# Prompt attention as half-array matmuls: 64 rows of the array for the scores, 64 columns for the values

## The chip, the cores and the metric

The kernel runs on one core of a Trainium2 chip. The metric is device time in microseconds, the median of several runs of the whole program. Three runs of the kernel before gave 1952.34 (median), 1952.07 and 1954.67 us.

The engines are named as in the profile: PE is the matrix engine, PEld its weight loads, DVE, ACT and POOL the vector, scalar and general engines, SP the queue that issues most of the transfers. A matmul multiplies a stationary operand (loaded as weights) with a moving operand that streams through it.

## The reference

One layer of a hybrid decoder is computed for a prompt of 256 tokens and for 8 single decode tokens: a half-step FFN, a mixing stage, a second half-step FFN, a final norm. Mixing has a group of attention heads beside a group of RWKV heads. The change touches the attention of the prompt:

```
qb = q.reshape(B, nb, BLOCK, N_KV_HEADS, GQA_GROUP, HEAD_DIM)
kc = concatenate([kp[:, :-1], kp[:, 1:]])      # the block before, and its own
s = einsum('...qhgd,...khd->...hgqk', q, k) * HEAD_DIM**-0.5 + bias
s = where(valid, s, -inf)
m = maximum(max(s), sink);  p = exp(s - m)
denom = sum(p) + exp(sink - m)
out = einsum('...hgqk,...khd->...qhgd', p / denom, v)
```

There are 16 query heads of 64 dimensions and 4 key/value heads, so four query heads share one key head. The 256 tokens form two blocks of 128. The second block's queries see 256 keys, the first block's only their own 128.

## The kernel before

The 264 columns of every activation are the 256 prompt tokens and the 8 decode tokens, and features lie along the 128 partitions. Every large product goes through `gemm`: weights come from memory as fp32, ACT makes a rounded copy `hi`, DVE the rest `lo`, and three matmuls of 264 columns (hi by hi, hi by lo, lo by hi) stand for one full product. These write the PSUM tiles called `acc`. All smaller products, attention among them, use plain fp32 operands and write PSUM tiles called `m`; each of them appears in the trace as two matmul records, one for each of the two passes that an fp32 matmul takes here.

The mixing stage multiplies by `w_in` tile by tile (`win`) in the order of the table `SEQ`: RWKV batches, then two key tiles and two value tiles (kind `kv`), then eight query tiles (kind `q`). Work that follows on a tile is a Python generator (`attend`, `prep`, `chain` and others) which moves forward one step at a time between chunks of the next `gemm` (`tick`). A scheduler then places every instruction on its engine with costs of its own, so the final order of the matmuls on PE is not the order in which the code is written.

A query tile `t` holds two heads, one in partitions 0 to 63 and one in 64 to 127 (`HALF`), and belongs to key pair `p = t // 4`. `attend(t, q)` does for it:

- scores (lines 796 to 798): for each head `h`, one matmul for the second block against 256 keys and one for the first block against 128 keys. The stationary operand is a block of `q` with all 128 partitions. So that only one head counts, the keys lie in two tiles per pair, `kT[p][0]` and `kT[p][1]`, each with the other head's 64 partitions set to zero (lines 926 to 931).
- bias, softmax and three transposes for each head (lines 799 to 816).
- values (lines 819 to 822): for each head, one matmul with the first 128 values for 256 queries and one with the second 128 values for the last 128 queries. The stationary operand is `Vt[p][:, i, :]` with the columns of both heads, so the output has 128 partitions of which 64 are wanted. ACT copies these out, one copy for each head (line 824).

Blocks that outlive a stage are taken by `blk(tag, n)` as `n` rows of 320 elements; block `y` has 16 elements more at its end. In the rows of the profile `kv` is the block that holds the keys and values, `o` the block that holds the `q` tiles, and the `t` in `m<-t,kv` are the probabilities.

Of the kernel before, what the change touches and what calls it, by code (L numbers as in the profile page):

```python
# [10 lines left out]
ALU = mybir.AluOpType  # L11
AX = mybir.AxisListType

P = 128
NP = 256
NB = 8
T = NP + NB
# [7 lines left out]
HALF = (slice(0, 64), slice(64, 128))  # L25
# [5 lines left out]
ROW = 320  # L31
# [21 lines left out]
def body(tc, I, O):  # L53
    nc = tc.nc
    V, A, G, TE, SP = nc.vector, nc.scalar, nc.gpsimd, nc.tensor, nc.sync
# [3 lines left out]
    def uid(s):  # L59
        cnt[0] += 1  # L60
        return f"{s}{cnt[0]}"

    def tt(e, out, a, b, op):
        return e.tensor_tensor(out=out, in0=a, in1=b, op=op)  # L64

    def stt(out, a, s, b, op0, op1):
        return V.scalar_tensor_tensor(out=out, in0=a, scalar=s, in1=b, op0=op0, op1=op1)  # L67
# [11 lines left out]
    def mm(out, lhsT, rhs, start=True, stop=True, **k):  # L79
        return TE.matmul(out, lhsT, rhs, start=start, stop=stop, **k)  # L80
# [16 lines left out]
    def spawn(g):  # L97
        tasks.append(g)
        return g

    def pause(n):
        for _ in range(n):
            yield

    with ExitStack() as ctx:
        cp = ctx.enter_context(tc.tile_pool(name="cp", bufs=1))
        sp = ctx.enter_context(tc.tile_pool(name="sp", bufs=1))
# [3 lines left out]
        cur = [None]  # L111

        def blk(tag, n, dt=F32):
            t = sp.tile([P, n * ROW + (16 if tag == "y" else 0)], dt, tag=tag, bufs=1, name=uid(tag))
            return [t[:, j * ROW:j * ROW + T] for j in range(n)]

        def pairs(*rows):
# [2 lines left out]
        def tmp(shape=(P, T), dt=F32):  # L120
            pool, n = cur[0]
            return pool.tile(list(shape), dt, tag="t", bufs=n, name=uid("t"))
# [4 lines left out]
        def mp():  # L127
            return pp.tile([P, 512], F32, tag="m", bufs=NM, name=uid("m"))
# [42 lines left out]
        def vc(i):  # L171
            return vec[:, i:i + 1]
# [189 lines left out]
        def mixing_body(mx, n2, n3, XD, XR):  # L362
            def fix(shape, name):
                return mx.tile(list(shape), F32, name=name)

            def ring(shape, tag, bufs):
                return mx.tile(list(shape), F32, tag=tag, bufs=bufs, name=uid(tag))

            def load(src, shape):
                t = ring(shape, "ld", NLD)  # L370
                SP.dma_start(t, src)
                return t
# [10 lines left out]
            rs = fix((P, T), "rs")  # L383
# [366 lines left out]
            kT, Vt = [None] * 2, [None] * 2  # L750
# [39 lines left out]
            def attend(t, q):  # L790
                p = t // 4
                G.tensor_copy(qd[:, p, :, t % 4], q[:, NP:T])
                bs = [load(I["bias"][(2 * p + h) * 4 + t % 4], (P, 256)) for h in range(2)]
                yield
                spp = [mp(), mp()]
                for h in range(2):
                    mm(spp[h][:, 0:256], q[:, P:NP], kT[p][h][:, 0:NP])
                    mm(spp[h][:, 256:384], q[:, 0:P], kT[p][h][:, 0:P])
                sc = [(tmp((P, 256)), tmp((P, P))) for h in range(2)]
                mxv = ring((P, 4), "mxv", 6)  # L800
                for h, sps in enumerate(spp):
                    s1, s0 = sc[h]
                    head = (2 * p + h) * 4 + t % 4
                    for s, a, b, j in ((s1, sps[:, 0:256], bs[h], 0), (s0, sps[:, 256:384], bs[h][:, P:256], 1)):
                        V.tensor_tensor_reduce(out=s, in0=a, in1=b, op0=ALU.add, op1=ALU.max, scale=1.0,  # L805
                                               scalar=vc(VSK + head), accum_out=mxv[:, 2 * h + j:2 * h + j + 1])
                softmax([x for y in sc for x in y], mxv, [vc(VSK + (2 * p + h) * 4 + t % 4) for h in range(2)], 4)
                yield
                yield from pause(PW[4])
                for s1, s0 in sc:  # L810
                    tp = mp()
                    TE.transpose(tp[:, 0:P], s0, ident)  # L812
                    TE.transpose(tp[:, P:2 * P], s1[:, 0:P], ident)  # L813
                    TE.transpose(tp[:, 2 * P:3 * P], s1[:, P:256], ident)  # L814
                    A.copy(s1, tp[:, 0:256])
                    V.tensor_copy(s0, tp[:, 256:384])
                yield
                pt = sc
                op = mp()
                for h in range(2):  # L820
                    mm(op[:, h * 256:h * 256 + 256], Vt[p][:, 0, :], pt[h][0], True, False)
                    mm(op[:, h * 256 + P:h * 256 + 256], Vt[p][:, 1, :], pt[h][1], False, True)
                for h in range(2):
                    A.copy(q[HALF[h], :NP], op[HALF[h], h * 256:h * 256 + 256])
                mixed[8 + t] = q

            sd = fix((P, P), "sd")
# [79 lines left out]
            for kind, i in SEQ:  # L907
                if kind == "b":
                    bt = newbatch(i)
                    for k in range(BATCH[i]):  # L910
                        p = bt.p0 + k
                        x = [shifted(2 + 3 * p + j, tmp()) for j in range(3)]
                        spawn(prep(p, bt, k, *x))
                    bat.append(spawn(chain(bt)))
                    bts.append(bt)
                    if len(bat) == len(BATCH):
                        A.dma_start(O["sh"], shc)
                elif kind == "kv":
                    w, p = i // 2, i % 2
                    ps = win(LKV + i)  # L920
                    if w:
                        xs = (tmp(),)
                        with tc.high_priority():
                            tt(V, xs[0], ps[:, :T], rs, ALU.mult)
                    else:
                        xs = (kvb[2 * p], kvb[2 * p + 1])
                        kT[p] = xs
                        for h in range(2):
                            G.memset(xs[h][HALF[1 - h], :], 0.0)
                            with tc.high_priority():  # L930
                                tt(V, xs[h][HALF[h], :], ps[HALF[h], :T], rs[HALF[h], :], ALU.mult)
                    spawn(kvtask(w, p, xs))
                else:
                    ps = win(LKV + 4 + i)
                    q = ob[i]
                    with tc.high_priority():
                        stt(q, ps[:, :T], 0.125, rs, ALU.mult, ALU.mult)
                    att.append(spawn(attend(i, q)))
                    if i % 4 == 3:
                        scores.append(spawn(dec_scores(i // 4)))  # L940
                    if len(att) == 8:
                        att.append(spawn(dec_attend(list(att), scores)))
# [19 lines left out]
            for pi, ks in enumerate(PASS):  # L962
# [15 lines left out]
                for o in range(KD):  # L978
                    ps = acc()
# [58 lines left out]
        kvb, ob, yb = blk("kv", 6), blk("o", 8), blk("y", 8)  # L1038
# [107 lines left out]
```

## Time and profile before

| what | value |
|---|---|
| median of three runs | 1952.34 us |
| the profiled execution | 1952.57 us |
| its span in the profile | 1950.8 us |
| PE busy | 1935.6 us |
| DVE busy | 1307.7 us |
| ACT busy | 1035.9 us |
| POOL busy | 260.2 us |

The span runs from the first to the last instruction; the profiled execution's own time is 1.77 us more. Times in the profile's rows count from the start of the span. The first FFN takes the time up to about 757 us, the mixing stage from there to about 1145 us, the second FFN the rest.

A row of a group reads: line, engine, operation, output and operands (the moving one first), for a matmul the rows by the columns of the array that are in use, the moving operand's shape, and the count; then busy time and the mean of one. The mean is the time from the start of a matmul to the end of its result, which is longer than the distance between two starts, because matmuls follow each other in a pipeline. For the cost of a matmul the distance between starts in the timeline is the measure.

### The profile page before, as it was taken

The numbers are of one execution on the slowest core, as the hardware profiler recorded it, in microseconds if no ns is written. First come the engines' busy times: TensorE is split into PE (matmuls) and PEld (weight loads), VectorE is DVE, ScalarE is ACT, GpSimd is POOL, SyncE is SP. The second block draws the span as 40 slices with busy tenths as digits, with TensorE's granted clock in tenths as the row PEclk, the third lists the DMA queues.
The fourth block names the chain that finished last, engine by engine and source line by source line (L and its number), as shares of the span: only waits on it lengthen the run. The fifth ranks groups of instructions, "written<-read, shape, count | busy, mean of one in ns | idle before, by whom it ended". The sixth has DMA issues, their size and how long they took to land.

```text
span 1950.8 us, 45522 instructions
## 1 busy us (share of the span) xinstructions
PE 1935.6 (99%) x17131; PEld 1919.6 (98%) x17131; DVE 1307.7 (67%) x2591; ACT 1035.9 (53%) x2069; POOL 260.2 (13%) x382
## 2 busy tenths in 40 slices
PE   9999999999999999999999999999999999999998
PEld 9999999999999999999999999999999999999998
DVE  5865555655556567799768877866666666666655
ACT  5644444444454456665577645644444444444445
POOL 0401101010010112231102100210101001010012
PEclk9999999999999999999999999999999999999999
DMA  7666666655656567555545655566666666666654
GB/s 241 178 195 193 185 195 197 184 188 178 189 182 186 183 194 232 165 169 157 149 128 163 188 157 183 175 186 188 190 192 193 186 193 189 192 193 184 194 180 149
DMA packets 220958, 358.10 MB, mean 184 GB/s; under 512 B 34866, under 2 KB 74434, under 8 KB 220738
## 3 DMA queue, kind: packets, MB, share of 16 engines
q1 hardware_dynamic: 214226, 346.59, 59.5%
q10 hardware_dynamic: 6512, 8.61, 1.4%
q8 instruction: 134, 2.20, 0.4%
q14 instruction: 86, 0.70, 0.1%
HBM read 347.48 MB, written 9.70 MB: 183 GB/s over the span
## 4 chain that ended last, share of the span: by engine, by line
PE 98%; DVE 1%; ACT 0%; DMA 0%; issue 0%; DVEq 0%; SPq 0%; ACTq 0%
PE acc L80 89%; PE m L80 8%; DMA x<-in_x 0%; DMA t<-dr 0%; DVE y L64 0%; PE m L535 0%; DVE lo L64 0%; ACT t L74 0%; ACT hi L137 0%; PE m L812 0%; PE m L493 0%; PE m L528 0%; PE m L813 0%; PE m L814 0%; DVE t L805 0%
## 5 line engine op out<-in xcount | busy, mean ns | idle before, releaser
L64 DVE TENSOR_TENSOR lo<-raw,hi 128x512 fp32r<-128x512 f32 (+1 forms) x1288 | 875.7, 683 | 523.4 <-ACT hi L137 496.2
L137 ACT CAST hi<-raw 128x512 fp32r<-128x512 f32 (+1 forms) x1288 | 777.1, 607 | 803.3 <-PE acc L80 735.5
L80 PE MATMUL acc<-x,hi 128*128 128x264 f32 x4840 | 900.0, 287 | 1.6 <-DVE st L64 1.3
L80 PEld LDWEIGHTS acc<-x,hi 128*128 128x128 f32 x4840 | 753.2, 189 | 4.9 <-ACT t L74 1.4
L80 PE MATMUL acc<-x,lo 128*128 128x264 f32 x2420 | 692.6, 286 | 0.2 <-DVE lo L64 0.2
L80 PE MATMUL acc<-h,hi 128*128 128x264 f32 x2752 | 495.1, 284 | 0.0
L80 PEld LDWEIGHTS acc<-x,lo 128*128 128x128 f32 x2420 | 458.5, 190 | 1.7 <-DVE lo L64 0.4
L80 PEld LDWEIGHTS acc<-h,hi 128*128 128x128 f32 x2752 | 424.4, 189 | 0.0
L80 PE MATMUL acc<-h,lo 128*128 128x264 f32 x1376 | 387.2, 284 | 0.0
L80 PEld LDWEIGHTS acc<-h,lo 128*128 128x128 f32 x1376 | 259.2, 189 | 0.0
L64 POOL TENSOR_TENSOR t<-t,t 128x264 f32<-128x264 f32 x74 | 80.3, 1085 | 1096.4 <-DVE t L64 950.3
L80 PE MATMUL acc<-y,hi 128*128 128x264 f32 x648 | 123.9, 285 | 0.0
L80 PE MATMUL acc<-o,hi 128*128 128x264 f32 x648 | 120.0, 283 | 0.0
L80 PE MATMUL acc<-kv,hi 128*128 128x264 f32 x582 | 109.8, 284 | 0.0
L80 PEld LDWEIGHTS acc<-y,hi 128*128 128x128 f32 x648 | 101.4, 189 | 0.1
L80 PEld LDWEIGHTS acc<-o,hi 128*128 128x128 f32 x648 | 100.1, 189 | 0.0
L67 DVE SCALAR_TENSOR_TENSOR x<-acc,x 128x264 f32<-128x264 f32 x192 | 81.0, 426 | 24.5 <-PE acc L80 23.6
L80 PE MATMUL acc<-y,lo 128*128 128x264 f32 x324 | 92.0, 284 | 0.0
L80 PE MATMUL acc<-o,lo 128*128 128x264 f32 x324 | 91.7, 283 | 0.0
L80 PEld LDWEIGHTS acc<-kv,hi 128*128 128x128 f32 x582 | 90.2, 189 | 0.1
L64 DVE TENSOR_TENSOR t<-acc,t 128x264 f32<-128x264 f32 x156 | 67.4, 432 | 33.1 <-PE acc L80 32.9
L80 PE MATMUL acc<-kv,lo 128*128 128x264 f32 x291 | 82.8, 284 | 0.0
(300 smaller groups left out, 1635.5 us busy)
## 6 DMA issues: line engine op xcount, KB each, us to landing
raw<-in_gu SPq DMA_DIRECT2D x688, 256.0 KB, 3.4
raw<-in_dn SPq DMA_DIRECT2D x224, 256.0 KB, 2.9
raw<-in_win SPq DMA_DIRECT2D x152, 256.0 KB, 3.4
raw<-in_dn SPq DMA_DIRECT2D x160, 192.0 KB, 2.7
raw<-in_wout SPq DMA_DIRECT2D x64, 256.0 KB, 3.4
xsp<-x ACTq DMA_DIRECT2D x16, 132.0 KB, 3.7
x<-xsp SPq DMA_DIRECT2D x16, 132.0 KB, 3.6
ld<-in_sT SPq DMA_DIRECT2D x16, 128.0 KB, 4.2
```

The lines of the kernel that those rows point to most:

```text
L64: return e.tensor_tensor(out=out, in0=a, in1=b, op=op)
L67: return V.scalar_tensor_tensor(out=out, in0=a, scalar=s, in1=b, op0=op0, op1=op1)
L80: return TE.matmul(out, lhsT, rhs, start=start, stop=stop, **k)
L137: A.copy(hi[:, :w], raw[:, :w])
```

## The change

Scores: a matmul reads only the 64 partitions of its head, from `q` and from a single key tile, so that it uses 64 rows of the array. Values: a matmul has only the 64 columns of its head as weights and writes only that head's 64 partitions, so that it uses 64 columns of the array. In both places the loop now goes over the column range first and over the two heads inside it. One ACT copy takes the finished 128 partitions out. The key tile of a pair is written whole, by one DVE multiplication, with no zeroed halves. The 16 spare elements lie behind block `e` in place of block `y`.

```
@@ blk @@
-            t = sp.tile([P, n * ROW + (16 if tag == "y" else 0)], dt, tag=tag, bufs=1, name=uid(tag))
+            t = sp.tile([P, n * ROW + (16 if tag == "e" else 0)], dt, tag=tag, bufs=1, name=uid(tag))
@@ attend @@
                 spp = [mp(), mp()]
-                for h in range(2):
-                    mm(spp[h][:, 0:256], q[:, P:NP], kT[p][h][:, 0:NP])
-                    mm(spp[h][:, 256:384], q[:, 0:P], kT[p][h][:, 0:P])
+                for a, b, n in ((0, P, NP), (NP, 0, P)):
+                    for h in range(2):
+                        r = HALF[h]
+                        mm(spp[h][:, a:a + n], q[r, b:b + P], kT[p][r, 0:n])
...
                 op = mp()
-                for h in range(2):
-                    mm(op[:, h * 256:h * 256 + 256], Vt[p][:, 0, :], pt[h][0], True, False)
-                    mm(op[:, h * 256 + P:h * 256 + 256], Vt[p][:, 1, :], pt[h][1], False, True)
-                for h in range(2):
-                    A.copy(q[HALF[h], :NP], op[HALF[h], h * 256:h * 256 + 256])
+                for i, a in ((0, 0), (1, P)):
+                    for h in range(2):
+                        r = HALF[h]
+                        mm(op[r, a:NP], Vt[p][:, i, r], pt[h][i], i == 0, i == 1)
+                A.copy(q[:, :NP], op[:, :NP])
@@ the keys @@
-                        xs = (kvb[2 * p], kvb[2 * p + 1])
-                        kT[p] = xs
-                        for h in range(2):
-                            G.memset(xs[h][HALF[1 - h], :], 0.0)
-                            with tc.high_priority():
-                                tt(V, xs[h][HALF[h], :], ps[HALF[h], :T], rs[HALF[h], :], ALU.mult)
+                        xs = (kvb[p],)
+                        kT[p] = xs[0]
+                        with tc.high_priority():
+                            tt(V, xs[0], ps[:, :T], rs, ALU.mult)
```

The scheduler puts the matmuls of the mixing stage in a new order. Three places on PE show what matters. A row gives the line, the operation, output and operands with running numbers, and the shape of the output; `m_...<-kv,o` is a score matmul (the two heads of a tile write two tiles with numbers of their own), `m_...<-t,kv` a value matmul, `acc` a matmul of a gemm. The score rows look alike before and after since their output has 128 partitions in both, but after the change each uses 64 rows of the array.

The first place is the second query tile's scores, before:

```order
L80 MATMUL m_13972<-C,t_13869 88x2 x3
L80 MATMUL m_14072<-kv_110,o_111 128x256
L80 MATMUL m_14072<-kv_110,o_111 128x128
L80 MATMUL acc_14326<-x_107,lo_14359 128x264
L80 MATMUL acc_14326<-x_107,hi_14358 128x264
L80 MATMUL m_14073<-kv_110,o_111 128x256
L80 MATMUL m_14073<-kv_110,o_111 128x128
L80 MATMUL m_14191<-sgl,ld_13858 128x264
```

And of the change:

```order
L80 MATMUL m_13966<-C,t_13863 88x2 x3
L80 MATMUL m_14066<-kv_110,o_111 128x256
L80 MATMUL m_14066<-kv_110,o_111 128x128
L80 MATMUL acc_14320<-x_106,lo_14323 128x264
L80 MATMUL acc_14320<-x_106,hi_14322 128x264 x2
L80 MATMUL acc_14320<-x_106,lo_14323 128x264
L80 MATMUL m_14067<-kv_110,o_111 128x256
L80 MATMUL m_14067<-kv_110,o_111 128x128
L80 MATMUL m_14185<-sgl,ld_13852 128x264
```

The two heads' matmuls still stand apart, with matmuls of the gemm between them, although the code alternates the heads.

The second place is the scores of the fifth query tile, before:

```order
L80 MATMUL acc_15319<-x_108,hi_15413 128x264
L80 MATMUL m_15381<-kv_110,o_111 128x256
L80 MATMUL m_15381<-kv_110,o_111 128x128
L80 MATMUL m_15382<-kv_110,o_111 128x256
L80 MATMUL m_15382<-kv_110,o_111 128x128
L80 MATMUL acc_15319<-x_108,hi_15413 128x264
```

And of the change:

```order
L493 MATMUL m_15341<-C,t_15113 128x128 x2
L80 MATMUL m_15371<-kv_110,o_111 128x256
L80 MATMUL m_15372<-kv_110,o_111 128x256
L80 MATMUL m_15371<-kv_110,o_111 128x128
L80 MATMUL m_15372<-kv_110,o_111 128x128
L80 MATMUL acc_15309<-x_108,hi_15403 128x264
```

Here the heads do alternate, and the four matmuls stand together.

The third place is the end of the first tile's values beside the fourth tile's scores, before:

```order
L80 MATMUL acc_14480<-x_109,lo_14617 128x264
L80 MATMUL m_14345<-t_13902,kv_110 128x128
L80 MATMUL m_14345<-t_13903,kv_110 128x256
L80 MATMUL m_14376<-kv_110,o_111 128x256
L80 MATMUL m_14376<-kv_110,o_111 128x128
L80 MATMUL m_14345<-t_13904,kv_110 128x128
L80 MATMUL m_14427<-qb_10433,ld_14428 128x2x4 x2
```

And of the change:

```order
L80 MATMUL acc_14473<-x_107,hi_14519 128x264 x2
L80 MATMUL m_14339<-t_13896,kv_110 64x128
L80 MATMUL m_14369<-kv_110,o_111 128x256
L80 MATMUL m_14339<-t_13898,kv_110 64x128
L80 MATMUL m_14369<-kv_110,o_111 128x128
L80 MATMUL m_14420<-qb_10433,ld_14421 128x2x4 x2
```

Matmuls on 64 columns and matmuls on 64 rows now take turns here, one at a time, between matmuls on the whole array.

## Prediction

> **What bounds the kernel now.** I read the page first (busy times), then a table by stage, then the waits, then the timeline of PE around the attention.
>
> ```profile
> PE 1935.6 (99%) x17131; PEld 1919.6 (98%) x17131; DVE 1307.7 (67%) x2591; ACT 1035.9 (53%) x2069; POOL 260.2 (13%) x382
> PE 98%; DVE 1%; ACT 0%; DMA 0%; issue 0%; DVEq 0%; SPq 0%; ACTq 0%
> 0.00:757.00 757.00, 755.45 (x6267) 754.66 (x6268) 464.76 (x788) 383.36 (x693) 98.01 (x107) 1.00 0.64 193
> 757.00:1145.00 388.00, 383.23 (x4244) 368.45 (x4243) 316.26 (x889) 252.57 (x654) 68.77 (x176) 0.99 0.56 161
> 1145.00:1951.00 806.00, 796.90 (x6624) 796.46 (x6623) 526.68 (x915) 399.93 (x723) 93.43 (x99) 1.00 0.62 186
> ```
>
> PE is busy for 99% of the span and makes up 98% of the chain that ended last. The mixing stage, the fourth line, is no exception: 383.23 of 388.00 us (the first number is the stretch, the second PE). So what the change does to the time is what it does to the length of PE's own queue in that stage, plus PE's few waits there:
>
> ```profile
> PE m L80 <- issue: 2.4, 1, 2.4
> PE acc L80 <- DVE st L64: 1.3, 1, 1.3
> PE m L80 <- ACT t L504: 1.1, 1, 1.1
> 943.80:947.20 3.40, 3.40 (x17) 3.40 (x17) 0.69 (x1) 1.44 (x4) 0.00 (x0) 0.50 0.53 152
> 1100.80:1104.20 3.40, 3.40 (x17) 3.40 (x16) 3.02 (x13) 1.69 (x4) 0.73 (x1) 0.50 0.38 117
> ```
>
> Three waits, 4.8 us together, and two stretches of 3.4 us in which the granted clock (the 0.50) is half, which lose about 1.7 us each: 8.2 us is all that better order in this stage could win back beyond PE's work.
>
> **Part 1, the matmuls themselves.** The attention of the prompt is these four groups, 128 records, two for each of 64 matmuls:
>
> ```profile
> L80 PE MATMUL m<-t,kv 128*128 128x256 f32 x32 | 10.0, 395 | 0.0
> L80 PE MATMUL m<-kv,o 128*128 128x256 f32 x32 | 9.8, 388 | 0.0
> L80 PE MATMUL m<-t,kv 128*128 128x128 f32 x32 | 6.7, 292 | 0.0
> L80 PE MATMUL m<-kv,o 128*128 128x128 f32 x32 | 6.1, 274 | 0.0
> ```
>
> Their place in PE's queue is read from starts, for one tile's scores:
>
> ```profile
> 978.20 0.28 PE L80 MATMUL acc<-x,lo 128*128 128x264 f32 x1
> 978.32 0.29 PE L80 MATMUL acc<-x,hi 128*128 128x264 f32 x1
> 978.44 1.47 PE L80 MATMUL m<-kv,o 128*128 128x256 f32 x8
> 979.67 0.37 PE L80 MATMUL acc<-x,hi 128*128 128x264 f32 x1
> 979.88 0.28 PE L80 MATMUL acc<-x,lo 128*128 128x264 f32 x1
> ```
>
> Starts of gemm matmuls lie 0.12 us apart. The second one after the scores starts at 979.88, so the scores take 979.88 - 0.12 - 978.44 = 1.32 us of the queue: four passes of 256 and four of 128 columns, 0.22 and 0.11 us each. One head's pair of matmuls is 0.66 us, a tile's scores and values 2.64 us, all eight tiles 21.1 us.
>
> Do two half-array matmuls run at once? The trace of before has such pairs, on 64 rows (`m<-kr,bk`) and on 64 columns (`m<-uv,BT`, `m<-gm,uv`):
>
> ```profile
> 815.98 0.63 PE L80 MATMUL m<-t,C 128*128 128x280 f32 x2
> 816.54 2.06 PE L80 MATMUL m<-kr,bk 64*128 64x128 f32 x32
> 818.53 0.39 PE L80 MATMUL acc<-x,hi 128*128 128x264 f32 x1
> 818.75 0.28 PE L80 MATMUL acc<-x,lo 128*128 128x264 f32 x1
> 891.30 0.22 PE L80 MATMUL m<-gm,W 64*64 64x64 f32 x1
> 891.44 1.15 PE L80 MATMUL m<-uv,BT 128*64 128x64 f32 x32
> 892.43 1.10 PE L80 MATMUL m<-gm,uv 128*64 128x64 f32 x32
> 893.46 0.51 PE L80 MATMUL acc<-x,hi 128*128 128x264 f32 x2
> 893.81 0.29 PE L80 MATMUL acc<-x,lo 128*128 128x264 f32 x1
> ```
>
> They do. 32 passes of 128 columns take 818.53 - 816.54 = 1.99 us; one after another they would take 32 x 0.11 = 3.5. The 64 passes of 64 columns take 893.46 - 891.44 = 2.02 us where 64 x 0.055 would be 3.5.
>
> But a pair has to stand together in PE's queue. In the new order the scores of tiles 1, 5 and 6 (counting from 1) stand as pairs, tile 8's only in the 256-column matmuls, and tiles 2, 3, 4 and 7 not at all: their heads are apart, as at the first of the three places shown. Of the values, three tiles stand as full pairs, two in their 256-column matmuls, one overlaps a 128-column one, two are all singles. A full pair saves one head, 0.66 us, a 256-column pair 0.44, a 128-column one 0.22. Scores: 3 x 0.66 + 0.44 = 2.42. Values: 3 x 0.66 + 2 x 0.44 + 0.22 = 3.08. Saved: **5.5 us** of a possible 10.6. A single half-array matmul saves nothing, since the time goes by the columns that stream through.
>
> **Part 2, the boundaries.** Changing the shape of the array in use costs time at both sides. Into `m<-kr,bk`: two passes of 280 columns (0.24 each) from 815.98 end at 816.46, the next start is 816.54, 0.08 late; sixteen slots of 0.11 would take 1.76, they took 1.99, 0.23 more; the first gemm matmul behind lasts 0.22 until the next start in place of 0.12, 0.10 more. That is 0.41 us for one entry and one exit. On columns: 0.14 between 891.30 and 891.44 in place of 0.055; 2.02 in place of 32 x 0.055 = 1.76; and from 893.46 to 893.81 two gemm starts in 0.35 in place of 0.24. That is 0.085 + 0.26 + 0.11 = 0.45 us. And single small matmuls between full-array values:
>
> ```profile
> 1005.74 0.59 PE L80 MATMUL m<-t,kv 128*128 128x256 f32 x2
> 1006.26 0.33 PE L80 MATMUL m<-BT,W 64*64 64x64 f32 x2
> 1006.52 0.92 PE L80 MATMUL m<-t,kv 128*128 128x128 f32 x4
> 1007.37 0.32 PE L80 MATMUL m<-gm,W 64*64 64x64 f32 x2
> 1007.63 0.49 PE L80 MATMUL m<-t,kv 128*128 128x128 f32 x2
> 1008.04 0.27 PE L80 MATMUL m<-BT,W 64*64 64x64 f32 x1
> ```
>
> From 1005.74 to 1008.04 are 2.30 us; the values are 1.32, the two small ones 0.11 each; 0.76 us is left for four boundaries and half of a fifth. So a boundary costs 0.17 to 0.22 us; I take 0.20, nearest to the 64-row and 64-column rows, which are the shapes that the change uses.
>
> I counted in both orders where neighbours on PE differ in shape and one of them is an attention matmul: 8 before (small matmuls among values, as just shown), 58 after. Of the 58, 22 lie between the whole array and 64 rows, 21 between the whole array and 64 columns, 8 between the two halves (the third place shown), 7 beside smaller shapes. Boundaries without attention: 72 before, 73 after. So 50 more, at 0.20 us: **10.0 us** lost, 8.5 to 11.0 by the bounds.
>
> [...]
>
> **Part 3, the rest.**
>
> ```profile
> L824 ACT COPY o<-m 64x256 f32<-64x256 f32 x16 | 5.9, 366 | 8.4 <-PE m L80 8.2
> L929 POOL MEMSET kv<- 64x264 f32 x4 | 1.2, 312 | 0.2
> L64 DVE TENSOR_TENSOR kv<-acc,rs 64x264 f32<-64x264 f32 x4 | 1.7, 418 | 0.1
> L80 PE MATMUL acc<-e,hi 128*128 128x264 f32 x194 | 39.1, 282 | 0.0
> L80 PE MATMUL acc<-y,hi 128*128 128x264 f32 x648 | 123.9, 285 | 0.0
> ```
>
> Half of the copies (2.9 us of ACT), all four memsets (1.2 us of POOL) and half of the key multiplications (0.8 us of DVE) go. PE hides all three: it works 383 of 388 us in the stage, and none of these lines ends one of its waits. Were that cover gone they would be worth 4.9 us at most. No wait and no transfer is added; the copy of the values now waits for both heads, and what reads it is only the later split of that tile into `hi` and `lo`. The padding moves block `e` by 64 bytes; matmuls that read `e` and `y` last the same (282 and 285 ns), so nothing.
>
> **Sum.** 1952.57 (the profiled execution) - 5.5 + 10.0 = 1957.1; by the bounds of the boundary price 1955.6 to 1958.1. The median of the runs is 0.2 lower than that execution: **1957 us**.
>
> **The rivals.**
>
> *Boundaries hidden (faster).* If a matmul on half of the array let the next shape's weights in while it streams, the extra boundaries would cost nothing and the 5.5 us stay: 1947; with every pair together, 1942. It decides once a boundary costs under 5.5/50 = 0.11 us. For it: only moving operands of 64 and 128 columns are shown beside such boundaries, the new ones have up to 256. Against it: the values of 256 columns at 1005.74 pay the boundary too. 12%.
>
> *PE's waits go (no change).* The order of the stage is new, and the three waits of 4.8 us and the half-clock stretches (3.4) hang on that order: `lo` behind the chain's steps on DVE, a copy on ACT. With some 5 of these 8.2 us gone, the loss is cancelled: 1952. For it: DVE and ACT lose work. Against it: they lose 0.8 and 2.9 us over 200, and the longest of the waits is put down to no engine. 25%.
>
> *Waits are added (slower still).* The same new order can make two or three more such waits of 1.1 to 2.4 us, or one more half-clock stretch: some 5 us on top, 1962. Likewise 1962 if the halves never overlap for 256 columns, so that the 5.5 us aren't saved. For it: PE is fed one chunk at a time in this stage, with DVE at 316 of 388 us. 13%.
>
> The forecast itself, with waits as before: 50%, its own range 1955.5 to 1958.5.
>
> **How the numbers follow.** Under 0.2% (3.9 us) can hardly be told from no change here, so faster is under 1948.4 and slower over 1956.2. Faster: the first rival, 12%. Within: the second, 25%, and the lower edge of the forecast, 4%: 29%. Slower: 59%. The range leaves out half of the first and part of the third rival: 1948.5 to 1963.
>
> **What would show it.** In the new profile paired scores should read 64 rows, with eight records in about 0.66 us and a boundary of 0.2 at each side; single ones 0.66 us for a head, plus boundaries. PE's time over the stage should grow by 4 to 5 us with the two FFNs unchanged. Wrong would be: starts of single half-array matmuls at their plain distance (first rival), or a stage that is longer or shorter mainly by idle time of PE or its clock (second and third).

## The result and the profile after

The changed kernel takes **1962.71 us** (median of 6 runs, 1961.49 to 1970.93) against 1952.66 of the kernel before (6 runs, 1952.07 to 1954.67): ratio **1.0058 [1.0048, 1.0068]**, 10 us slower. The forecast was slower by 4.5 us. The profiled execution took 1963.6 us (span 1961.8), 11.0 us more than that of before; the working below goes by these two.

The table by stage comes first, split where the first FFN's last matmul that reads `h` starts and where the second FFN's first one does, so that the stages compare exactly. The columns are as in the prediction: the stretch, PE busy, PEld, DVE, ACT, POOL, granted clock, DMA share, GB/s. Before:

```profile
0.00:750.80 750.80, 749.25 (x6216) 748.47 (x6217) 461.30 (x783) 380.35 (x688) 96.50 (x105) 1.00 0.64 192
750.80:1286.30 535.50, 530.73 (x5464) 515.75 (x5463) 426.52 (x1074) 334.54 (x807) 91.67 (x200) 0.99 0.57 168
1286.30:1942.30 656.00, 655.36 (x5456) 655.27 (x5454) 416.21 (x732) 320.60 (x575) 69.90 (x74) 1.00 0.62 185
```

And after:

```profile
0.00:750.90 750.90, 749.88 (x6217) 749.03 (x6218) 461.39 (x783) 380.39 (x688) 94.93 (x101) 1.00 0.64 192
750.90:1298.70 547.80, 541.04 (x5463) 516.51 (x5462) 425.52 (x1072) 329.70 (x796) 91.64 (x200) 0.98 0.56 164
1298.70:1953.30 654.60, 653.96 (x5456) 653.87 (x5454) 416.27 (x732) 320.48 (x575) 69.85 (x74) 1.00 0.62 186
```

The middle stage grew by 12.4 us (from 535.4 to 547.8, by the starts themselves), and the second FFN became 1.4 us shorter. The sum is the 11.0. In the middle stage PE sits idle for 547.80 - 541.04 = 6.76 us where it was 4.77, so 2.0 us are waits. PE's busy time grew by 10.3, and its mean clock fell from 0.99 to 0.98.

The granted clock comes next: first the four stretches of after in which it is half, then two windows that lie just ahead of such a stretch:

```profile
942.20:945.60 3.40, 3.40 (x46) 3.16 (x48) 1.77 (x4) 0.77 (x2) 0.20 (x1) 0.50 0.46 136
990.00:996.80 6.80, 6.80 (x34) 6.80 (x34) 4.43 (x17) 4.04 (x15) 0.19 (x1) 0.50 0.43 124
1078.70:1082.10 3.40, 3.40 (x18) 3.40 (x18) 3.12 (x16) 1.37 (x3) 0.00 (x0) 0.51 0.83 238
1112.90:1119.70 6.80, 6.80 (x33) 6.80 (x33) 4.35 (x16) 2.21 (x10) 1.26 (x3) 0.50 0.13 39
1109.48:1112.90 3.42, 3.42 (x27) 2.67 (x27) 2.65 (x15) 0.67 (x2) 0.00 (x0) 1.00 0.58 185
986.60:990.00 3.40, 3.40 (x25) 2.53 (x24) 2.41 (x12) 1.74 (x7) 0.24 (x1) 1.00 0.42 117
```

Before had 6.8 us of half clock; after has 20.4. At half clock the starts of gemm matmuls lie 0.22 us apart in place of 0.12, so about half of the added 13.6 us is lost: **6.8 us**. And in the two windows ahead (986.6 and 1109.48) PE is busy for all 3.40 us: no wait sets off the stretches at 990 and 1112.9.

PE's longest waits after:

```profile
PE acc L80 <- issue: 1.7, 1, 1.7
PE acc L80 <- DVE lo L64: 1.1, 1, 1.1
...
PE m L80 <- ACT BT L540: 0.9, 1, 0.9
PE m L80 <- DMA ld<-in_kc: 0.9, 1, 0.9
PE m L80 <- DVE gm L64: 0.7, 1, 0.7
```

None is as long as the 2.4 us of before, but there are more of them.

The attention's groups now read 64 rows and 64 columns, and one tile's scores stand as pairs in the timeline:

```profile
L80 PE MATMUL m<-kv,o 64*128 64x256 f32 x32 | 9.0, 428 | 1.6 <-ACT BT L540 0.9 <-DVE gm L64 0.7
L80 PE MATMUL m<-t,kv 128*64 128x256 f32 x32 | 7.1, 405 | 0.0
L80 PE MATMUL m<-kv,o 64*128 64x128 f32 x32 | 5.8, 284 | 0.0
L80 PE MATMUL m<-t,kv 128*64 128x128 f32 x32 | 5.4, 285 | 0.0
```

```profile
1050.85 0.38 PE L493 MATMUL m<-C,t 128*128 128x128 f32 x2
1051.16 0.92 PE L80 MATMUL m<-kv,o 64*128 64x256 f32 x8
1052.02 0.39 PE L80 MATMUL acc<-x,hi 128*128 128x264 f32 x1
1052.24 0.29 PE L80 MATMUL acc<-x,lo 128*128 128x264 f32 x1
```

The two matmuls at 1050.85 take 0.11 each, so the scores could start at 1051.07 and start 0.09 late. Eight records paired are 0.66 us, so the next start could be 1051.82 and is 0.20 late; the first gemm matmul then takes 0.22 in place of 0.12. That is 0.39 us for one entry and one exit, 0.195 a boundary. (The starts are measured; that eight paired records take 0.66 us is the prediction's figure.)

At the place where the two shapes take turns:

```profile
986.34 0.40 PE L80 MATMUL acc<-x,hi 128*128 128x264 f32 x2
986.68 0.43 PE L80 MATMUL m<-t,kv 128*64 128x128 f32 x2
987.04 0.70 PE L80 MATMUL m<-kv,o 64*128 64x256 f32 x2
987.66 0.43 PE L80 MATMUL m<-t,kv 128*64 128x128 f32 x2
988.03 0.48 PE L80 MATMUL m<-kv,o 64*128 64x128 f32 x2
988.44 1.06 PE L80 MATMUL m<-qb,ld 128*128 128x8 f32 x8
```

(Records with the same names are merged in a row: `m<-kv,o` at 987.04 has 256 columns, at 988.03 it has 128.) Two gemm matmuls end their slots at 986.58; the four singles need 0.22 + 0.44 + 0.22 + 0.22 = 1.10 us, and the next work starts at 988.44. The other 0.76 us are four boundaries and half of a fifth, 0.17 each. Singles save nothing, as forecast.

### The profile page after: what moved, and what is told of

The parts are those of the page before. It is cut to its first block, busy times and chain, and to the rows that moved or that the text cites. A ratio compares the mean times of both kernels' runs of the same rounds, so it can differ in the third digit from the quotient of the medians.

```text
span 1961.8 us, 45497 instructions
## 1 busy us (share of the span) xinstructions
PE 1945.1 (99%) x17131; PEld 1919.5 (98%) x17131; DVE 1306.8 (67%) x2589; ACT 1031.0 (53%) x2059; POOL 258.6 (13%) x378
## 4 chain that ended last, share of the span: by engine, by line
PE 96%; DVE 1%; DMA 1%; ACT 1%; issue 0%; POOL 0%; SPq 0%; DVEq 0%; ACTq 0%; POOLq 0%
PE acc L80 88%; PE m L80 8%; DVE lo L64 0%; DMA t<-dr 0%; ACT t L74 0%; DMA ld<-in_kc 0%; DVE y L64 0%; DMA out_vp<-t 0%; DVE t L806 0%; DMA raw<-in_wout 0%; PE m L535 0%; DVE t L67 0%; DMA ld<-in_bias 0%; ACT hi L137 0%; PE m L813 0%
## 5 line engine op out<-in xcount | busy, mean ns | idle before, releaser
L64 POOL TENSOR_TENSOR t<-t,t 128x264 f32<-128x264 f32 x74 | 79.9, 1079 | 1096.0 <-DVE t L64 949.8
```

## The experiments

Each of the following kernels is the changed one with one edit, unless it says "before with". The numbers in the table at the end of this section put them side by side.

**Heads held together.** The four score matmuls of a tile, and its four value matmuls, are held together on PE.

```
-                for a, b, n in ((0, P, NP), (NP, 0, P)):
+                with tc.tile_critical():
+                  for a, b, n in ((0, P, NP), (NP, 0, P)):
...
-                for i, a in ((0, 0), (1, P)):
+                with tc.tile_critical():
+                  for i, a in ((0, 0), (1, P)):
```

> The changed kernel with the four score matmuls of a query tile held together on PE as one unit, and the four value matmuls too. All 64 now stand in 16 runs of four, so every pair of heads can overlap (10.6 us saved against the kernel before, where the changed kernel saves 5.5), and there are 32 shape boundaries beside attention in place of 58 (24 more than before, 4.8 us at 0.20). Theory A (part of the 10 us lost is the granted clock, which halves for 3.4 us when a stretch holds mostly single half-array matmuls and tiny ones): about 1947 us, faster than before, and no more half-clock time than before's 6.8 us (the changed kernel has 20.5). Rival B (the shapes themselves are dearer than I priced, the clock is incidental): boundaries of 0.35 us and more, 1950 to 1953, with the clock as in the changed kernel. Rival C (the loss is waits that the new order brings, shapes matter little): 1955 or more, since a unit of four holds PE until all four can start.

Measured: 1983.12 us, ratio 1.0156 [1.0141, 1.0171]. Every pair stands together, and the kernel is slower than all others here but the one with added work. Of the three forecasts only the one that went by waits held, and theory A's clock (no more than 6.8 us at half) didn't. PE waits for 27.2 us in the middle stage, and 37.5 us run at half clock. Its longest waits:

```profile
PE m L80 <- DMA x<-xsp: 2.9, 1, 2.9
PE m L80 <- DMA ld<-in_bias: 2.6, 1, 2.6
PE m L80 <- DMA sa<-gm: 2.3, 1, 2.3
```

The pairs do what they promise in PE's queue (table below); what holds them together costs several times that.

**Scores alone, values alone.** First the values as before, then the scores and keys as before.

```
-                for i, a in ((0, 0), (1, P)):
-                    for h in range(2):
-                        r = HALF[h]
-                        mm(op[r, a:NP], Vt[p][:, i, r], pt[h][i], i == 0, i == 1)
-                A.copy(q[:, :NP], op[:, :NP])
+                for h in range(2):
+                    mm(op[:, h * 256:h * 256 + 256], Vt[p][:, 0, :], pt[h][0], True, False)
+                    mm(op[:, h * 256 + P:h * 256 + 256], Vt[p][:, 1, :], pt[h][1], False, True)
+                for h in range(2):
+                    A.copy(q[HALF[h], :NP], op[HALF[h], h * 256:h * 256 + 256])
```

> Only the scores on 64 rows and the keys as one block; the values use the whole array as before. By the order on PE: 2.6 us saved in pairs, 24 more boundaries (4.8 us): plus 2.2 us of shape. Theory A: if the monitor behind the clock goes by the rows of the array in use, single score matmuls count half and extra half-clock stretches of 3.4 us come on top (1.7 us each): 1956 to 1959. Rival B: 1957 or more with the clock as before. Rival C: anything, by waits of PE.

> Only the values on 64 columns; scores and the zeroed key tiles as before. By the order on PE: 3.3 us saved in pairs, 28 more boundaries (5.3 us): plus 2.0 us of shape, 1954.5. Theory A with a monitor that goes by rows: all 128 rows are in use, so no more half-clock time than before: 1954 to 1956. With a monitor that goes by the area in use: extra half-clock stretches as with the scores, 1956 to 1959. Rival C: anything, by waits of PE.

(The monitor in these two forecasts is an assumption: the traces show a granted clock of 1.00 or 0.50, and no monitor.)

Measured: scores alone 1955.77 us, ratio 1.0012 [1.0003, 1.0022], with 10.2 us of half clock; values alone 1961.73 us, ratio 1.0046 [1.0031, 1.0061], with 17.0 us of half clock and 9.4 us of idle PE in the middle stage. By shapes the two are alike (24 and 29 boundaries more than before, 2.6 and 3.3 us saved). What makes them differ by 6 us is waits and clock: of the 8.3 us between the middle stages of the two profiled executions, 5.2 are idle time of PE and 2.8 the clock.

Scores alone had one more stretch of 3.4 us than before, as forecast by rows, and stayed 0.2 us under the forecast time. Values alone missed: its attention uses all 128 rows everywhere, so by rows it should have had no more than 6.8 us of half clock and at most 1956 us. One of its stretches follows a window in which PE was busy throughout:

```profile
989.45:992.85 3.40, 3.40 (x25) 2.82 (x24) 3.40 (x16) 2.89 (x14) 0.32 (x1) 1.00 0.63 211
992.87:996.27 3.40, 3.40 (x45) 3.16 (x44) 0.74 (x3) 3.40 (x15) 0.25 (x1) 0.51 0.78 221
```

So a new order, without one more matmul on 64 rows, can bring nearly as much half clock as the change did (17.0 us beside 20.4). The ten runs of scores alone show the clock's price without any change of the order: 1959.52 us at a mean granted clock of 0.993, 1951.54 us at 0.997.

**Rows, columns and the clock.** The kernel before with six stretches of added matmuls in the second FFN, 20 large ones each with small ones between them: on the whole array; on 64 rows, one at a time; on 64 columns; on 64 rows with both halves in turns; on 64 rows and 64 columns; on 64 rows without the small ones. This work is added; nothing reads its result.

```
+        def probe(s):
...
+            r, c = [(every, every), (lo, every), (every, lo), (lo, every), (lo, lo), (lo, every)][s]
+            for i in range(20):
+                keep(mm(a[c, :256], C[r, c], C[r, P:3 * P]))
+                if s == 3:
+                    keep(mm(b[:, :256], C[hi, 0:P], C[hi, P:3 * P]))
+                for j in range((1, 1, 2, 1, 2, 0)[s]):
+                    keep(mm(a[c, 256:264], C[r, c], C[r, P:P + 8]))
```

> The kernel before, with six added stretches of matmuls in the second FFN, one before the ninth output tile of each of its six parts; their results are not used. Each stretch repeats 20 times a 256-column matmul and small ones of 8 columns of the same shape: (1) whole array, (2) 64 rows, one half only, (3) 64 columns, one half only, (4) 64 rows, both halves at once, (5) 64 rows and 64 columns, one quarter, (6) 64 rows, one half only, without the small ones. Streaming columns fill about 0.65 of the time in (1) to (5), all of it in (6). Theory A by rows: the clock halves in (2) and (5) and stays full in (1), (3), (4), and in (6), whose share is 0.5. By area: it halves in (2), (3) and (5). Rival B and C: shape has no bearing on the clock, it stays full in all six. Each 256-column matmul of a single half should take 0.44 us as on the whole array, and a pair of halves in (4) 0.44 us together.

Measured (one run, 2048.04 us), by the table of windows for the six stretches in order; of the second and fifth, the part at half clock:

```profile
1309.00:1322.00 13.00, 13.00 (x83) 12.00 (x82) 1.43 (x3) 0.62 (x1) 0.00 (x0) 1.00 0.21 60
...
1451.70:1467.00 15.30, 15.30 (x49) 13.12 (x48) 0.00 (x0) 0.00 (x0) 0.00 (x0) 0.50 0.00 0
1591.00:1604.00 13.00, 13.00 (x117) 9.92 (x117) 1.05 (x3) 0.46 (x1) 0.00 (x0) 1.00 0.16 49
1726.00:1739.00 13.00, 13.00 (x121) 11.83 (x119) 0.82 (x2) 0.23 (x1) 0.00 (x0) 1.00 0.15 43
...
1864.70:1882.00 17.30, 17.30 (x85) 11.90 (x82) 0.00 (x0) 0.00 (x0) 0.00 (x0) 0.50 0.00 1
2005.00:2013.00 8.00, 8.00 (x38) 6.93 (x39) 1.27 (x3) 1.24 (x3) 0.74 (x1) 1.00 0.31 95
```

PE is busy all the time in each of them. The clock reads 0.50 where 64 rows are used one at a time among small matmuls, with 64 columns or with 128; it reads 1.00 on the whole array, on 64 columns with all 128 rows, on paired 64 rows, and on single 64 rows without the small ones. This is the forecast by rows in all six stretches. So in this run the clock goes with the rows of the array in use times the share of time that columns stream.

The stretches of half clock in the middle stages of these kernels last whole multiples of 3.41 us (3.41, 6.83, 20.48 and 23.89 us), and so do the times between them. So I cut the time into windows of 3.41 us along these edges; this is a way to count, and no trace shows that the clock goes by such windows. For each window I added up the columns that stream, each weighted by rows in use over 128, and divided by the some 8,000 that fit (an estimate: fp32 matmul records of 128 columns, counted as 256, mostly start 108 to 110 ns apart in the trace of before, about 8,010 in 3.41 us at 109; the divisor is the same for all windows). An fp32 column counts twice, since 256 of them take 0.22 us where 264 columns of a gemm take 0.12, and matmuls that run side by side are added:

```
window from      rows x streaming   rows x columns x streaming   half clock next
after   1109.5        0.41                0.22                     yes
after    986.6        0.34                0.27                     yes
after   1075.3        0.35                0.35                     yes
after   1048.0        0.42                0.42                     no
before   936.9        0.46                0.25                     no
before  1097.4        0.35                0.35                     yes
whole-array scores  1109.1   0.55         0.36                     no
```

By the area of the array (the last but one column) these seven would be mixed up.

The same count over all 2,055 windows at full clock between 750 and 1286 us of the twelve kernels (with the added stretches, to 2035 us) shows the same. All 30 windows below 0.38 are followed by half clock, none of those above 0.42 is, and of the 8 between, 2 are: these traces don't part the two kinds of window more sharply. By streaming alone a window of 0.87 is followed by half clock and one of 0.42 isn't. In 9 of the 32 windows ahead of half clock PE is busy throughout.

The stretch at 1112.9 needs care: the window ahead of it (0.41, and 0.41 by streaming alone) holds no matmul on 64 rows at all, but values on 128 rows among matmuls of 8 columns.

**Scores over the whole array, in the changed kernel's order.** Only the rows in use differ: the order of every engine is the same. The scores then add the other head's rows, so this kernel computes something else.

```
-                        r = HALF[h]
-                        mm(spp[h][:, a:a + n], q[r, b:b + P], kT[p][r, 0:n])
+                        mm(spp[h][:, a:a + n], q[:, b:b + P], kT[p][:, 0:n])
```

> The changed kernel, but each score matmul reads all 128 partitions of q and of the key tile (so a score is the sum over both heads of a tile, which is not what the reference computes). Every engine's instructions stand in exactly the changed kernel's order; only the score matmuls use 128 rows in place of 64. Shape: 22 boundaries fewer (minus 4.4 us), the pairs of scores lost (plus 2.4): minus 2 us. Theory A (clock by rows in use): the half-clock stretches at 990 and 1079 us, whose preceding 3.4 us hold single 64-row scores, go: half-clock time from 20.5 to about 10 us, minus 5 us; with the shape about 1955.5. Rival B (shape alone, clock by chance or by waits): 1960 to 1961, half-clock time 20 us as before. Rival C (waits): the order is the same, so hardly any gain, 1960 or more.

Measured: 1958.76 us, ratio 1.003 [1.0019, 1.0042], 4 us below the changed kernel. The windows in which the changed kernel fell to half clock:

```profile
986.60:990.00 3.40, 3.40 (x22) 2.51 (x22) 3.40 (x17) 2.65 (x12) 0.63 (x1) 1.00 0.55 160
990.00:996.80 6.80, 6.80 (x59) 6.66 (x58) 6.51 (x26) 5.54 (x21) 0.80 (x3) 1.00 0.53 157
1092.00:1095.40 3.40, 3.40 (x17) 3.40 (x17) 2.15 (x8) 1.73 (x4) 0.00 (x0) 0.50 0.47 163
1109.50:1112.90 3.40, 3.40 (x27) 2.67 (x27) 2.13 (x11) 1.09 (x3) 0.73 (x1) 1.00 0.41 123
```

The stretch at 990 is gone, as are those at 1079 and 1113; one at 1092 is new, behind a wait of 2.9 us for a transfer (`ld<-in_kc`), and the one at 942 is twice as long. Half clock falls from 20.4 to 10.2 us, as forecast by rows, and 22 boundaries go; the time lies between the two forecasts, since PE's idle time grew from 6.8 to 9.5 us.

By the count the scores' 64 rows made the stretches at 990 and 1079, 10.2 us: the windows ahead of them hold score matmuls on 64 rows and reach 0.34 and 0.35, where the same columns on 128 rows would count 0.43, just above the 0.42 beyond which no window is followed by half clock, and 0.54. (The second window also holds 0.9 us of idle time.) They did not make the stretch at 1113. There the values run 1.3 us earlier in this kernel, so the window of 3.41 us cuts the work at another place and reaches 0.55.

**Nothing on halves.** Scores as in the last one, and the values on whole columns as well, with the new loops and the one copy; this too computes something else, since each head's values overwrite rather than fill their half.

```
-                        mm(op[r, a:NP], Vt[p][:, i, r], pt[h][i], i == 0, i == 1)
-                A.copy(q[:, :NP], op[:, :NP])
+                        mm(op[:, h * 256 + a:h * 256 + 256], Vt[p][:, i, :], pt[h][i])
+                A.copy(q[:, :NP], op[:, P:P + NP])
```

> As the run before, and the value matmuls use all 128 columns too, each overwriting instead of accumulating, with one copy of 128 partitions that takes columns of both heads (the values are not what the reference computes). The new loops, the single key tile, the single copy and nearly the changed kernel's order, but no half-array matmul is left: 78 boundaries as in the kernel before (80). Theories A and B: what remains against the kernel before is the order and its waits, 1952 to 1955, half-clock time 7 to 10 us. Rival C (the loss is the order's waits): 1960 or more.

Measured: 1952.66 us, ratio 0.9996 [0.9987, 1.0005], with 6.8 us of half clock as before. The loss is gone with the half-array matmuls. The order on PE is nearly that of the changed kernel, not quite, and the waits shrank too (5.1 us idle, 9.5 in the kernel with whole scores), so the run doesn't part the matmuls from the waits. This kernel has the padding behind `e`, so the kernel to compare it with is the next one, the padding alone: 1952.66 beside 1950.75 us, with intervals that overlap, and middle stages of 535.2 and 535.4 us. The loops, the single key tile, the copy and the dropped memsets bring nothing and cost at most some 2 us.

**The padding alone.** Before with the 16 elements behind `e`, the order of every engine unchanged.

```
-            t = sp.tile([P, n * ROW + (16 if tag == "y" else 0)], dt, tag=tag, bufs=1, name=uid(tag))
+            t = sp.tile([P, n * ROW + (16 if tag == "e" else 0)], dt, tag=tag, bufs=1, name=uid(tag))
```

> The kernel before with only the 16 spare elements moved from block y to block e. Every engine's order is that of the kernel before. All theories: 1952 to 1954, no difference.

Measured: 1950.75 us, ratio 0.9987 [0.9978, 0.9996]: 0.13% faster than before and 12 us faster than the changed kernel. No forecast had a difference here, and it is the fastest of all kernels. The middle stage is unchanged (535.4 us) and the second FFN 1.4 us shorter:

```profile
1286.30:1940.90 654.60, 653.96 (x5456) 653.87 (x5454) 416.71 (x732) 320.43 (x575) 69.27 (x74) 1.00 0.62 186
```

The matmuls of the second FFN that read `y`, from the table of windows for that tile alone (the second number is PE's busy time), before and then with the padding moved:

```profile
1295.00:1940.00 645.00, 115.96 (x840) 107.98 (x840) 0.00 (x0) 7.87 (x16) 0.00 (x0) 1.00 0.62 186
```

```profile
1295.00:1940.00 645.00, 114.90 (x840) 106.73 (x840) 0.00 (x0) 8.02 (x16) 0.00 (x0) 1.00 0.62 186
```

The same 840 matmuls take 1.06 us less. Start by start, 130 of the 840 took 128 or 129 ns until the next start in place of 120, and with the padding moved none does, in the changed kernel neither. Two more kernels ask what about the address matters.

> The kernel before without any padding; the order of every engine is the same. Theory A (what counts is the address at which block y lies, moved by 64 bytes where the padding is behind e): y lies as in the kernel before, so about 130 of the 840 matmuls of the second FFN that read y again take 128 or 129 ns between starts in place of 120, and the second FFN lasts 656.0 us. Theory B (what lies behind y counts, or the 16 elements at y's own end): without them no matmul takes 128 ns, and the second FFN lasts 654.6.

> The kernel before with the padding behind y and behind e; the order of every engine is the same. Theory A (y's address): y lies as with the padding behind e, so all 840 matmuls that read y take 120 ns between starts and the second FFN lasts 654.6 us. Theory B (the 16 elements at y's own end, or what they move behind it): 128 and 129 ns show again, 656.0 us.

Measured, one run each: 1962.89 us without padding, 1952.86 with both. Both theories fell. Without padding every stage is longer:

```profile
0.00:755.50 755.50, 753.21 (x6216) 752.41 (x6217) 461.35 (x783) 380.14 (x688) 96.98 (x105) 1.00 0.63 191
755.50:1293.20 537.70, 531.84 (x5464) 516.24 (x5463) 426.14 (x1074) 334.31 (x807) 91.86 (x200) 0.99 0.56 167
1293.20:1952.50 659.30, 658.66 (x5456) 658.57 (x5454) 416.18 (x732) 320.49 (x575) 69.76 (x74) 1.00 0.61 184
```

In its first FFN 564 matmuls that read `x` take 126 ns between starts, and all distances together are 4.7 us beyond 120 each; in its second FFN matmuls take 126 whatever block they read. With both paddings 70 matmuls of the second FFN that read `e` take 127 or 128, 55 that read `y` take 126, and that stage lasts 655.7 us.

With both paddings the middle stage has no half clock at all, and yet lasts 535.7 us:

```profile
751.20:1286.90 535.70, 531.56 (x5462) 516.34 (x5461) 426.31 (x1074) 333.66 (x806) 90.99 (x200) 1.00 0.57 168
```

Its gemm matmuls are slower there: of 3,131 distances between their starts 1,040 are 120 ns, where the kernel before has 2,434 of 3,111; together they are 6.7 us beyond 120 each, against 2.8. So an offset of 64 bytes in what lies behind moves the time by up to 10 us (12.1 lie between no padding and the padding behind `e`, of which 1.6 are clock and waits of the middle stage), but which operand's address it is, and by what rule, stays open.

These kernels also show how far the half clock moves by itself. The order of every engine is that of the kernel before, and the middle stage has 6.8 us of it in the kernel before, 6.8 with the padding moved, 10.2 without padding and none with both.

**Scores together, values as before.** Holding the four value matmuls makes them wait for the softmax of both heads, so here only the scores are held.

```
+                with tc.tile_critical():
+                  for a, b, n in ((0, P, NP), (NP, 0, P)):
...
+                for h in range(2):
+                    mm(op[:, h * 256:h * 256 + 256], Vt[p][:, 0, :], pt[h][0], True, False)
```

> The changed kernel's scores, with the four score matmuls of a tile held together on PE, and the values as before (whole array, two copies); padding behind e. All eight tiles' scores are pairs (8 x 0.66 = 5.3 us saved) and there are 20 boundaries more than before (100 against 80), at 0.19 us 3.8 us. Ledger theory (time = queue of PE by shapes + PE's waits + half of the half-clock time + padding): -5.3 + 3.8 - 1.4 (padding, as seen in the second FFN) = -2.9 us, so 1950.5 beside a before of 1953.4, if waits and half-clock time stay those of before (6.0 us of idle PE in all, 6.8 us of half clock), and in any case a stage that fits the ledger within 1 us once its own idle and half-clock times are put in. Rival (holding PE for four makes waits by itself, as with values and scores held in the first run): idle PE grows by over 5 us, half-clock time with it, and the kernel is slower than before by 5 us or more.

Measured: 1976.96 us, ratio 1.0117 [1.01, 1.0134]; the rival was right. PE waits for 21.8 us in the middle stage and 41.0 us run at half clock, the longest stretch, 23.9 us, right behind a wait of 2.4 us that ends at 1124.1. The two longest waits, then that stretch:

```profile
PE m L80 <- DMA sa<-gm: 4.1, 1, 4.1
PE m L80 <- DVE Xt L64: 3.7, 1, 3.7
```

```profile
1124.20:1148.10 23.90, 23.90 (x152) 21.19 (x153) 11.04 (x48) 7.59 (x27) 3.04 (x7) 0.50 0.11 30
```

So holding the scores is enough to make the waits; the softmaxes aren't needed for it. Which step is late first under it was not followed further. (The profiled execution took 1982.48 us, so the table below shows this kernel at its slowest.)

**All of them side by side**, the middle stage alone, in us. "Rest" is what remains of the difference to before once PE's idle time and half of the half-clock time (less idle time within it) are taken off; "shapes" is what the prediction's two prices give for that kernel's order, 0.20 for each boundary more than the 80 of before, less the savings of its pairs.

```
kernel                   stage   idle  half clock   rest   shapes
before                   535.4    4.8     6.8        0       0
changed                  547.8    6.8    20.4      +3.6    +4.7
heads held together      566.6   27.2    37.5      -5.2    -5.6
scores alone             538.4    4.2    10.2      +2.4    +2.2
values alone             546.7    9.4    17.0      +2.6    +2.5
scores whole             543.4    9.5    10.2      +2.0    +2.7
nothing on halves        535.2    5.1     6.8      -0.6    -0.4
padding alone            535.4    5.6     6.8      -0.2     0
scores held together     566.7   21.8    41.0      -2.1    -1.3
```

The two prices hold within 1.1 us in all nine kernels. By the same sum the rest is +0.4 us without padding and +4.4 with both paddings, at no more boundaries: this is the slower gemm shown above, which the two prices don't know.

## Why the prediction was half right

**Part 1, pairs: right.** The halves run at once where they stand together, also for 256 columns (eight records from 1051.16, next start at 1052.02, where one after another would take 1.32 us), and singles save nothing. With every pair together the rest is 5.2 us below before, where the pairs' 10.6 less 25 boundaries give 5.6.

**Part 2, boundaries: right.** 0.195 and 0.17 us at the two places shown, against 0.20. By the prediction's own counts (58 and 73 against 8 and 72) there are 51 more boundaries, not 50, worth 0.2 us. Parts 1 and 2 together were forecast at +4.5; +3.6 is what is left of the measured difference once waits and clock are taken off.

**Part 3, the cover: right.** With no matmul on halves, the removed copies, memsets and multiplications gain nothing (1952.66 us, against 1950.75 with the padding alone).

**Part 3, "the padding ... so nothing": wrong by 1.4 us**, a gain. It compared mean durations (282 and 285 ns), although it takes the distance between starts as the measure of cost everywhere else. The step was in the trace of before in just that measure: 130 of the 840 matmuls that read `y` start the next one 8 or 9 ns late, 1.06 of the 1.4 us.

**The sum's tacit term, "with waits as before", failed.** It was taken as nothing for waits and for the clock. The waits cost 2.0 us, a little less than the two or three waits of 1.1 to 2.4 us that the third rival had; the clock cost **6.8 us**, and this is the term that made the sum wrong. The prediction had quoted both half-clock stretches of before, and used them only as something to win back, and in the third rival as "one more half-clock stretch", 1.7 us. There were 13.6 us more, and for most of it the cause isn't the one that this rival gave (PE fed one chunk at a time, hence waits): ahead of the stretches at 990 and 1112.9 PE was busy for all 3.40 us. Half-row score matmuls, which the prediction had counted as neutral but for their boundaries, bring windows with little streaming down to where half clock followed: by the count of the windows from 0.43 to 0.34 and from 0.54 to 0.35, ahead of the stretches at 990 and 1079, 10.2 of the 13.6 us or 5.1 of the 6.8. The other 3.4 us belong to the stretch at 1113, which is longer than its counterpart at 1100.8 of before; its window has no half-row matmul, and how much of it the change's new order made, and how much where the window happened to fall, stays open.

So: 3.6 for shapes (the remainder; by the prices 4.7), 6.8 for the clock, 2.0 for waits, 1.4 gained by the padding make the 11.0 us between the two profiled executions. The clock's loss isn't peculiar to the profiled execution: the six runs of after have a mean granted clock of 0.990 to 0.994, the lowest in the slowest run, and the runs of before beside the experiments 0.995 to 0.997.

Of the rivals, hidden boundaries and waits that go fell. The third gave nearly the measured time, 1962, for two reasons of which one is false (the halves do overlap) and the other too small and for the most part of another origin. That 1962.7 lies just inside the wide range, 1948.5 to 1963, is therefore luck. Shown by runs are the prices, that rows bear on the clock (0.50 and 1.00 in the added stretches), and the padding's effect. That rows made 5.1 us of the clock's loss rests on the count of the windows and on the run with whole scores, in which the windows also moved. Why the waits differ from order to order (4.2 to 27.2 us) is only listed, not explained.

## What to carry to other kernels

Half-array matmuls paid here only where both halves stood next to each other (by the prices 0.66 us saved by a full pair, nothing by singles), and each stay at another shape had to win back two boundaries of 0.2 us; in an order that a scheduler makes, count both before writing the change, and be wary of forcing the pairs by holding the engine: in both kernels that did so PE's idle time was 17 us or more above that of before, for pairs worth 5.3 and 10.6 us. Where PE's work was thin already (many small matmuls), using 64 rows in place of 128 also went with the lower clock (0.50 against 1.00 in the added stretches): add up rows times streaming for each 3.4 us there, not idle gaps. And when blocks move in memory, compare distances between starts matmul by matmul, since 64 bytes were worth about as much here as all the pairs together.

## What the runs showed of the hardware

- Counted over 3.41 us as rows in use times streaming, all 30 windows below 0.38 are followed by half clock, 2 of 8 between 0.38 and 0.42, none above. In the one run with added stretches the clock was 0.50 on 64 rows alone among small matmuls and 1.00 on 64 columns with all rows.
- Two half-row fp32 matmuls of 256 columns start 6 to 7 ns apart and then run side by side: a tile's eight score records, four of 256 and four of 128 columns, take 0.86 us to the next start with their boundaries (1051.16 to 1052.02 in the changed kernel), 1.32 before.
- The offset of blocks in memory changed a gemm's start distance from 120 to 126 or 128 ns for some of its matmuls, up to 10 us for the whole kernel (1950.75 us with the padding behind `e`, 1962.89 in the one run with none).
